# VectorE takes the weight sums of the first three feed-forward pairs, and the last row tile gets its residual from VectorE

## The chip, the cores and the metric

The kernel runs on one core of one Trainium2 chip. The metric is device time in microseconds (us). The kernel before took 1179.04 us as the median of three runs (1177.97 to 1402.14).

## The reference

The reference is one layer of a decoder trunk on 1024 positions of width 1024, all in float32. A first half computes latent attention, a short convolution and a state-space mixer from one normalised input and writes them through one output projection. What this document touches is the second half:

```
x = x + rms_norm(mixed, norm_mix_post)
h = rms_norm(x, norm_ffn_pre)
u = causal_dwconv(h @ ffn_w_up, ffn_conv_w) + ffn_conv_b      # 1024 -> 2 * 2816
gate, up = split(u)
x = x + rms_norm((silu(gate) * up) @ ffn_w_down, norm_ffn_post)
```

## The kernel before

Every float32 product is made of three TensorE products of rounded parts: a matrix is cast on ScalarE to a high part, the difference of matrix and high part is its low part, and high*high, high*low and low*high are summed in a PSUM bank. A low part is thus one elementwise subtraction per 128x1024 weight tile, after a cast.

**The up projection** works on pairs: pair j is gate tile j (`rg`) and up tile j (`ru`), each 128x1024 of weights. Instead of eight half products a pair takes seven, of sums and differences of weight halves (named 11, 12, S1, S2, S3, S4, 22) and of sums of activation halves (11, 21, T1, T2, T3, T4, 22), in the manner of Strassen and Winograd. So between load and product stand sums of weight halves (function `ew`, L1001), a cast on ScalarE, and the subtraction for the low part (L97 in `split_w`, L999 in `low`).

The first three pairs (j = 0, 1, 2; `NE` = 3) overlap the end of the first half, where rows 6 and 7 of the eight row tiles still pass through their norms (`norms`, L892). They go in steps over all three pairs: `pair_first` (L1040) makes the products 11 and 12 and gathers them in `ug`: ScalarE copies the first bank (L1045) and VectorE adds the second (L1048), which frees that bank. Then `sab_weights` (L1006) loads both tiles of the pair again, makes two sums of 128x512 in `ru`, and casts and lowers `ru`; S1 and S2 follow for all three pairs, first on one half of the columns, then on the other. Then `scd_weights` (L1013) loads the tiles a third time and makes the weights of S3, S4 and 22: four sums of 128x512 on VectorE, then casts and low parts, of which one is 128x512 (`hl_`) and one 128x1024 (`wlo`). In `sab_weights` the two sums and the low part of pairs 0 and 1 are on GpSimd (POOL) and those of pair 2 on VectorE; in `scd_weights` the two low parts of pairs 0 and 1 are on POOL and those of pair 2 on VectorE. The low parts of the first weights (`first_weights`, L972) are on POOL too.

The raw weight tiles rotate over three buffers (`raw` twice, `xraw` once), so the load of a tile waits on SyncE's queue until the low part or sum that last read its buffer is done.

The order of the instructions on each engine up to here is set by a planner that takes ready work by program order with costs of its own. From L1122 on TensorE, ScalarE, VectorE and SyncE follow the program's order (`by_hand`): pairs 3 to 21, then the down projection. POOL has nothing to do there but the last stores.

**The end.** The residual, x after the first half, was stored to the output rows by ScalarE's queue (`x2_st`, L925) long before. In the down projection row tile t is gathered in `acc[t]`. When a tile is complete, ScalarE squares its halves with a running sum (`squares`, L1357), VectorE and ScalarE make the reciprocal root (`scales`, L1361), VectorE multiplies by it and by the gain `gfin` (`finish`, L1369), and POOL issues a DMA (L1371) that adds the tile to the output rows in memory. Tiles 4 to 7 end one after the other at L1427 to L1433; for tile 7 the multiplication and the adding DMA go in two halves.

Of the kernel before, what the change touches and what calls it, by code (L numbers as in the profile page):

```python
# [8 lines left out]
F32 = mybir.dt.float32  # L9
# [4 lines left out]
ALU = mybir.AluOpType  # L14
# [3 lines left out]
D = 1024  # L18
# [26 lines left out]
def trunk(ctx: ExitStack, tc: tile.TileContext, x, xt, pos, cp, cst, amask, gains, wqkv, win, wqn, wqr, wkn,  # L45
          wv, wout, wup, wdn, out):
    nc = tc.nc
    pe, act, dve, pool, sp = nc.tensor, nc.scalar, nc.vector, nc.gpsimd, nc.sync

    def newpool(stack, name, bufs=1, **kw):  # L50
        if kw.get("space") is not DRAM:
            kw.setdefault("reuse_waits", "tile")
        return stack.enter_context(tc.tile_pool(name=name, bufs=bufs, **kw))
# [21 lines left out]
    def load_raw(src, w=1024):  # L75
        if more and more[2] % 3 == 2:
            raw = more[0].tile([128, 1024], F32, name="xraw")
        else:
            raw = wst.tile([128, 1024], F32, name="raw", bufs=2)
        if more:  # L80
            more[2] += 1
        sp.dma_start(out=raw[:, 0:w], in_=src)
        return raw
# [3 lines left out]
    def split_w(raw, w=1024, eng=None):  # L87
        if more and more[1] % 4 == 3:
            hi = more[0].tile([128, 1024], F32R, name="xhi")
            lo = more[0].tile([128, 1024], F32R, name="xlo")  # L90
        else:
            hi = wst.tile([128, 1024], F32R, name="whi", bufs=3)
            lo = wst.tile([128, 1024], F32R, name="wlo", bufs=3)
        if more:
            more[1] += 1
        act.copy(hi[:, 0:w], raw[:, 0:w])  # L96
        (eng or pool).tensor_tensor(out=lo[:, 0:w], in0=raw[:, 0:w], in1=hi[:, 0:w].bitcast(F32), op=ALU.subtract)  # L97
        return hi, lo
# [26 lines left out]
    def rsqrt_act(sp_, v, n, tag, bufs=2):  # L125

        y = sp_.tile([128, n], F32, name=tag + "_y", bufs=bufs)
        t = sp_.tile([128, n], F32, name=tag + "_t", bufs=bufs)
        act.activation(t, v, AF.Sqrt)
        dve.reciprocal(out=y, in_=t)  # L130
        dve.tensor_tensor(out=t, in0=y, in1=y, op=ALU.mult)
        dve.scalar_tensor_tensor(out=t, in0=t, scalar=-0.5, in1=v, op0=ALU.mult, op1=ALU.mult)
        dve.scalar_tensor_tensor(out=y, in0=t, scalar=1.5, in1=y, op0=ALU.add, op1=ALU.mult)
        return y
# [71 lines left out]
    with ExitStack() as g0:  # L206
# [8 lines left out]
        for k in range(KD):  # L215
# [12 lines left out]
            for c in parts:  # L228
                act.activation(hh[:, k, c], xr[:, c], AF.Copy, scale=g)
                dve.scalar_tensor_tensor(out=hl[:, k, c], in0=xr[:, c], scalar=g, in1=hh[:, k, c].bitcast(F32),  # L230
                                         op0=ALU.mult, op1=ALU.subtract)
# [37 lines left out]
    with ExitStack() as g2:  # L269
        st = newpool(g2, "st2")  # L270
        tb = st.tile([32, T], F32, name="tb")
# [16 lines left out]
        for i, n in enumerate((256, 128)):  # L288
            dve.scalar_tensor_tensor(out=v2[:, i, :], in0=cq_ss[:, i * NT:(i + 1) * NT], scalar=1.0 / n, in1=r2,
                                     op0=ALU.mult, op1=ALU.mult)  # L290
# [5 lines left out]
        for t in range(NT):  # L296
            dve.tensor_scalar(out=craw[:, t, 0:256], in0=craw[:, t, 0:256], scalar1=rc[:, t:t + 1], scalar2=None,
                              op0=ALU.mult)
            dve.tensor_scalar(out=craw[:, t, 256:384], in0=craw[:, t, 256:384], scalar1=rc[:, NT + t:NT + t + 1],
                              scalar2=None, op0=ALU.mult)  # L300
        for i in range(3):
            g = par("qn", i) if i < 2 else par("kvn")
            for hf in range(2):
                pt = bank()
                for q in range(4):
                    tr = pe.transpose(pt[:, q * 128:(q + 1) * 128], craw[:, hf * 4 + q, i * 128:(i + 1) * 128], ident)
                    if first_tr is None:
# [5 lines left out]
                                         op1=ALU.subtract)  # L313
# [66 lines left out]
    for d in (11, 9, 7, 5, 3, 1):  # L380
# [8 lines left out]
                             op0=ALU.mult, op1=ALU.mult)  # L389
# [13 lines left out]
    for i in range(6):  # L403
        u = in_tile(win[i], last_sq if i == 2 else None)
        if i == 1:
            tc.add_manual_dep(first_tr.ins, marks[2].ins.name,
                              mybir.DependencyInfo(mybir.DependencyClass.NoSync, mybir.DependencyReason.DATA),
                              reason="the norms of c_q and c_kv take that long")
        acc = ut.tile([128, T], F32, name="acc", bufs=1)
# [10 lines left out]
    with ExitStack() as g4:  # L420
        st = newpool(g4, "st4")
        tb = [st.tile([128, T], F32, name=f"tb{i}") for i in range(2)]
# [32 lines left out]
    for c in range(NT):  # L455
# [6 lines left out]
        for h in range(4):  # L462
            dve.scalar_tensor_tensor(out=dg[:, h, :], in0=aB[:, h, :], scalar=acs[:, c * 4 + h:c * 4 + h + 1],
                                     in1=maskT, op0=ALU.subtract, op1=ALU.add)
# [4 lines left out]
        for i in range(2):  # L469
# [3 lines left out]
                          in1=dtv[:, c, :].unsqueeze(2).broadcast_to([128, 4, 64]), op=ALU.mult)  # L473
# [6 lines left out]
        for g in range(2):  # L480
# [3 lines left out]
                          in0=psc[:, 0:256].rearrange("p (g l) -> p g l", g=2).unsqueeze(2).broadcast_to(  # L484
                              [128, 2, 2, 128]),
                          in1=dg.rearrange("p (g r) l -> p g r l", g=2), op=ALU.mult)
        if c > 0:
            Cd = sd.tile([128, 4, 128], F32, name="Cd")
            dve.tensor_tensor(out=Cd.rearrange("p (g r) l -> p g r l", g=2),
                              in0=Cm[:, :, cs].unsqueeze(2).broadcast_to([128, 2, 2, 128]),  # L490
                              in1=eB.rearrange("p (g r) l -> p g r l", g=2), op=ALU.mult)
# [19 lines left out]
        for i in range(2):  # L511
            dve.scalar_tensor_tensor(out=yz[:, i, cs], in0=xs[:, i, cs], scalar=par("dsk", i),
                                     in1=py[:, i * 128:(i + 1) * 128], op0=ALU.mult, op1=ALU.add)
# [3 lines left out]
        for i in range(2):  # L517
            pe.matmul(py[:, 256:258], sq[:, i, :], ones, start=i == 0, stop=i == 1)
        dve.tensor_scalar(out=vs[:, c:c + 1], in0=py[:, 256:257], scalar1=1.0 / 256, scalar2=EPS, op0=ALU.mult,
                          op1=ALU.add)  # L520
    rs = rsqrt(small, vs, NT, "rs")
    col_to_rows(rs, NT, small, rB2 := sd.tile([128, T], F32, name="rB2"), "r2")
    for i in range(2):
        dve.scalar_tensor_tensor(out=y[6 + i], in0=yz[:, i, :], scalar=par("sdn", i), in1=rB2, op0=ALU.mult,
                                 op1=ALU.mult)
# [3 lines left out]
    for i in range(2):  # L529
# [3 lines left out]
        acc = ut.tile([128, T], F32, name="acc", bufs=1)  # L533
# [266 lines left out]
    x2_st = {}  # L800
# [23 lines left out]
    H0, H1 = slice(0, 512), slice(512, 1024)  # L824
# [144 lines left out]
    def half(w, c):  # L969
        return [v_[:, c].rearrange("p (k c) -> p k c", k=4) for v_ in w]  # L970

    def first_weights(j, rg):  # L972
        ta = split_w(rg)
        return {"11": half(ta, H0), "12": half(ta, H1)}

    wts = [first_weights(j, load_raw(wup[j])) for j in range(NE)]
# [5 lines left out]
    def raws(j):  # L982
        ru = load_raw(wup[NJ + j])
        return load_raw(wup[j]), ru
# [10 lines left out]
    def half_split():  # L995
        return (ft.tile([128, 512], F32R, name="hh_", bufs=2), ft.tile([128, 512], F32R, name="hl_", bufs=2))

    def low(eng, lo, src, hi):
        eng.tensor_tensor(out=lo, in0=src, in1=hi.bitcast(F32), op=ALU.subtract)  # L999

    def ew(eng, dst, a_, b_, op):  # L1001
        eng.tensor_tensor(out=dst, in0=a_, in1=b_, op=op)  # L1002
# [3 lines left out]
    def sab_weights(w, rg, ru, eng):  # L1006

        ew(eng, ru[:, H0], ru[:, H0], ru[:, H1], ADD)
        ew(eng, ru[:, H1], ru[:, H0], rg[:, H0], SUB)
        tb = split_w(ru, eng=dve if w is wts[2] else pool)  # L1010
        w.update({"S1": half(tb, H0), "S2": half(tb, H1)})

    def scd_weights(w, rg, ru):  # L1013

        eng = dve if w is wts[2] else pool
        s1 = ft.tile([128, 512], F32, name="s1")
        ew(dve, s1, ru[:, H0], ru[:, H1], ADD)
        ew(dve, ru[:, H0], rg[:, H0], ru[:, H0], SUB)
        ew(dve, s1, s1, rg[:, H0], SUB)
        ew(dve, rg[:, H1], rg[:, H1], s1, SUB)  # L1020
        d_ = half_split()
        act.copy(d_[0], rg[:, H1])
        low(eng, d_[1], rg[:, H1], d_[0])
        c_ = split_w(ru, eng=eng)
        w.update({"S3": half(c_, H0), "22": half(c_, H1), "S4": half(d_, H0)})
# [51 lines left out]

    fst = [pair_first(j, wts[j]) for j in range(NE)]
    for j in range(NE):
        sab_weights(wts[j], *raws(j), pool if j < 2 else dve)  # L1080
    for nm in ("T1", "T2", "22", "T3", "T4"):
        if nm == "T4":
            put("T4", t4, 4)
# [42 lines left out]
    rg, ru = raws(NE)  # L1126
    for j in range(NE - 1, NJ):
# [38 lines left out]
        if more_:  # L1166
# [30 lines left out]
            if j < NJ - 2:  # L1197
                rg, ru = raws(j + 2)
# [21 lines left out]
    acc = [ab.tile([128, D], F32, name=f"acc{t}") for t in range(NT)]  # L1220
# [63 lines left out]
    def tok(ps, t, ol, or_, start, stop, more_):  # L1284
        ts = slice(t * 128, (t + 1) * 128)
        for i, (l_, r_) in enumerate(((ol[0], or_[0]), (ol[0], or_[1]), (ol[1], or_[0]))):
            pe.matmul(ps[t], l_[:, ts], r_[:, H1], start=start and i == 0, stop=stop and i == 2,  # L1287
                      skip_group_check=more_)
# [48 lines left out]
    fin = None  # L1337
# [10 lines left out]
    def gather(ps, t, row, c, copy):  # L1348
        dst = acc[row + t][:, c]
        if copy:  # L1350
            act.copy(dst, ps[t])
        else:
            ew(dve, dst, ps[t], dst, ADD)

    FULL = slice(0, 1024)
# [5 lines left out]
    def scales(t, n=1):  # L1361
        v = fin.tile([128, 4], F32, name="fv", bufs=2)[:, 0:n]
        ew(dve, v, ssd_[:, t:t + n, 0], ssd_[:, t:t + n, 1], ADD)
        dve.tensor_scalar(out=v, in0=v, scalar1=1.0 / D, scalar2=EPS, op0=ALU.mult, op1=ALU.add)
        return rsqrt_act(fin, v, n, f"fr{n}")

    def finish(t, r, *cs):
        for c in cs:
            dve.scalar_tensor_tensor(out=acc[t][:, c], in0=acc[t][:, c], scalar=r, in1=gfin[:, c], op0=ALU.mult,  # L1369
                                     op1=ALU.mult)  # L1370
            st_ = pool.dma_start(out=out[t * 128:(t + 1) * 128, c], in_=acc[t][:, c], accum_op=ALU.add)  # L1371
            tc.add_manual_dep(st_.ins, x2_st[t].ins.name,
                              mybir.DependencyInfo(mybir.DependencyClass.Sync, mybir.DependencyReason.DATA),
                              reason="the rows are added to what lies there")

    prepare_to(-2)
    act.copy(last[2][:, H0], b_last)
# [4 lines left out]
    for k, (bk_, q_, p_) in enumerate(steps):  # L1382
# [19 lines left out]
        if not ci and q_ == "P7" and p_ == ch[0]:  # L1402
# [3 lines left out]
            fin = newpool(ds_, "fin")  # L1406
            gfin = fin.tile([128, D], F32, name="gfin")
# [5 lines left out]
        if ci and q_ == "P7":  # L1413
# [4 lines left out]
            elif i == 2:  # L1418
                r = scales(0, 4)
# [2 lines left out]
                finish(i - 2, r[:, i - 2:i - 1], FULL)  # L1422

    ps = bank["b"]
    for t in range(4):
        squares(4 + t, H1)
    for t in range(4):  # L1427
        for p_ in ch:
            tok(ps, t, O[4, 0, p_], O[2, 1, p_], False, p_ == ch[-1], True)
        gather(ps, t, 4, H0, False)  # L1430
        squares(4 + t, H0)
        r = scales(4 + t)
        finish(4 + t, r, *((FULL,) if t < 3 else (H1, H0)))  # L1433
    by_hand.close()
    ds_.close()

# [81 lines left out]
```

## Time and profile before

| | |
|---|---|
| median of three runs | 1179.04 us |
| lowest run | 1177.97 us |
| profiled execution, own time | 1176.4 us |
| its span, first to last instruction | 1174.6 us |
| granted TensorE clock, mean | 0.988 |
| TensorE busy | 1126.3 us |
| VectorE busy | 887.6 us |
| ScalarE busy | 579.9 us |
| POOL busy | 167.7 us |

The profile is of one execution. Busy time is per engine; "idle before" is what an engine waited just ahead of an instruction, with what ended that wait. Times of the timeline count from the span's first instruction. A granted clock of 1.00 is 2.4 GHz, one of 0.50 is 1.2 GHz.

### The profile page before, as it was taken

What the parts mean: (1) busy time and instruction counts of PE and PEld (TensorE: products, weight loads), DVE (VectorE), ACT (ScalarE), POOL (GpSimd) and SP (SyncE); (2) the same over time, 40 slices, a digit from 0 to 9 for tenths busy, and PEclk for the clock granted to TensorE, in tenths of its full rate; (3) what the DMA queues carried; (4) which work ended last, traced back from release to release, by engine and by line L of the source; (5) the groups of instructions that cost most, each with busy time, mean ns of one, the idle gap of its engine ahead of it and who ended that gap; (6) DMA issues with size and microseconds to landing.
All of it is one profiled execution on the core that took longest, in us unless ns stands there. A gap on an engine that the chain in (4) does not pass through costs nothing.

```text
span 1174.6 us, 14711 instructions
## 1 busy us (share of the span) xinstructions
PE 1126.3 (96%) x5548; PEld 942.1 (80%) x5548; DVE 887.6 (76%) x1374; ACT 579.9 (49%) x931; POOL 167.7 (14%) x100
## 2 busy tenths in 40 slices
PE   9999999999999999979899999999999998999995
PEld 8778877788888877868688888888888887788884
DVE  4687378667889765876987777887878678779975
ACT  5743233157777744634544454444444444543542
POOL 2322211134424113341100000000000000000002
PEclk9999999999999999989999999999999999999998
DMA  8531151130111256551223132222222290560008
GB/s 270 190 91 45 36 167 41 48 96 10 37 28 28 72 207 198 188 175 40 90 90 108 55 107 74 88 90 73 90 72 90 70 360 26 190 232 1 1 4 140
DMA packets 42823, 118.01 MB, mean 100 GB/s; under 512 B 5392, under 2 KB 7040, under 8 KB 42400
## 3 DMA queue, kind: packets, MB, share of 16 engines
q1 hardware_dynamic: 37856, 104.36, 27.6%
q0 software_dynamic: 1296, 4.19, 2.2%
q10 hardware_dynamic: 3600, 8.52, 2.0%
q8 instruction: 43, 0.70, 0.3%
q14 instruction: 28, 0.23, 0.1%
HBM read 94.59 MB, written 22.47 MB: 100 GB/s over the span
## 4 chain that ended last, share of the span: by engine, by line
PE 63%; DVE 7%; issue 5%; DMA 4%; POOL 2%; ACT 2%; SPq 0%; POOLq 0%; ACTq 0%; DVEq 0%
PE cb L1032 26%; PE pb L1287 7%; PE pc L1287 5%; PE tp L1032 4%; PE S L104 2%; PE pt L705 2%; PE S L105 2%; PE S L106 2%; PE cb L105 2%; PE cb L104 2%; PE cb L106 2%; DMA raw<-in_wup 1%; PE po L721 1%; PE po L720 1%; DVE a L655 1%
## 5 line engine op out<-in xcount | busy, mean ns | idle before, releaser
L1032 PE MATMUL cb<-a,whi 128*128 128x512 f32 (+1 forms) x712 | 215.1, 384 | 5.2 <-DVE ug L1002 4.2
L1032 PEld LDWEIGHTS cb<-a,whi 128*128 128x128 f32 x712 | 133.3, 191 | 30.9 <-DVE ug L1002 4.6
L1032 PE MATMUL cb<-a,wlo 128*128 128x512 f32 (+1 forms) x356 | 136.7, 384 | 2.5 <-POOL wlo L97 2.5
L97 POOL TENSOR_TENSOR wlo<-raw,whi 128x1024 fp32r<-128x1024 f32 (+1 forms) x29 | 70.5, 2433 | 267.6 <-ACT whi L96 247.4
L1371 POOL DMA_DIRECT2D out<-acc x9 | 8.0, 907 | 596.7 <-DVE acc L1369 596.5
L106 PE MATMUL bk<-hh,wlo 128*128 128x512 f32 x224 | 89.3, 399 | 0.0
L104 PE MATMUL bk<-hh,whi 128*128 128x512 f32 x224 | 89.2, 398 | 0.0
L105 PE MATMUL bk<-hl,whi 128*128 128x512 f32 x224 | 89.0, 397 | 0.0
L1032 PEld LDWEIGHTS cb<-a,wlo 128*128 128x128 f32 x356 | 67.9, 191 | 15.9 <-POOL wlo L97 3.3
L363 DVE SCALAR_TENSOR_TENSOR cg<-ug,cpt,cg 128x1023 f32<-128x1023 f32 (+1 forms) x46 | 61.0, 1325 | 15.9 <-ACT cg L1114 12.9
L1032 PE MATMUL cb<-a,xhi 128*128 128x512 f32 (+1 forms) x248 | 72.7, 376 | 0.0
L96 ACT CAST whi<-raw 128x1024 fp32r<-128x1024 f32 (+1 forms) x33 | 33.8, 1025 | 65.5 <-PE bk L105 34.9
L363 DVE SCALAR_TENSOR_TENSOR cu<-uu,cpt,cu 128x1023 f32<-128x1023 f32 (+1 forms) x42 | 53.8, 1281 | 9.5 <-ACT cu L1114 8.8
L999 DVE TENSOR_TENSOR wlo<-raw,whi 128x1024 fp32r<-128x1024 f32 x35 | 42.7, 1222 | 13.3 <-ACT whi L1131 5.1
L1032 PEld LDWEIGHTS cb<-a,xhi 128*128 128x128 f32 x248 | 45.5, 188 | 8.4
L1114 ACT ACTIVATE cg<-ug,cpt 128x1024 f32<-128x1024 f32 x19 | 23.7, 1245 | 57.0 <-DVE ug L1002 54.8
L106 PEld LDWEIGHTS bk<-hh,wlo 128*128 128x128 f32 x224 | 42.2, 188 | 9.7 <-issue 0.4
L105 PEld LDWEIGHTS bk<-hl,whi 128*128 128x128 f32 x224 | 42.2, 188 | 9.4 <-issue 0.2
L104 PEld LDWEIGHTS bk<-hh,whi 128*128 128x128 f32 x224 | 42.2, 188 | 9.1
L1249 ACT CAST oh<-x 128x1024 fp32r<-128x1024 f32 x31 | 31.9, 1052 | 35.2 <-PE pb L1287 21.9
L1032 PE MATMUL cb<-a,xlo 128*128 128x512 f32 (+1 forms) x124 | 46.9, 378 | 1.4 <-DVE xlo L999 1.4
L999 DVE TENSOR_TENSOR ol<-x,oh 128x1024 fp32r<-128x1024 f32 x31 | 37.2, 1219 | 13.4 <-ACT oh L1249 13.3
(568 smaller groups left out, 3078.5 us busy)
## 6 DMA issues: line engine op xcount, KB each, us to landing
raw<-in_wup SPq DMA_DIRECT2D x35, 512.0 KB, 3.7
x<-g_d SPq DMA_DIRECT2D x44, 256.0 KB, 5.4
x<-in_wdn SPq DMA_DIRECT2D x44, 256.0 KB, 5.4
g_d<-uu SPq DMA_DIRECT2D x20, 512.0 KB, 2.9
xraw<-in_wup SPq DMA_DIRECT2D x18, 512.0 KB, 3.9
raw<-in_win SPq DMA_DIRECT2D x14, 512.0 KB, 3.5
raw<-in_wout SPq DMA_DIRECT2D x13, 512.0 KB, 4.2
xk<-in_x SPq DMA_DIRECT2D x8, 512.0 KB, 6.0
```

Of the source, the lines that this page charges most:

```text
L96: act.copy(hi[:, 0:w], raw[:, 0:w])
L97: (eng or pool).tensor_tensor(out=lo[:, 0:w], in0=raw[:, 0:w], in1=hi[:, 0:w].bitcast(F32), op=ALU.subtract)
L104: pe.matmul(ps, ah, bh, start=start, stop=False)
L105: pe.matmul(ps, ah, bl, start=False, stop=False)
L106: return pe.matmul(ps, al, bh, start=False, stop=stop)
L363: dve.scalar_tensor_tensor(out=dst[:, s:T], in0=u[:, 0:T - s], scalar=par(wname, i * width + width - 1 - s), in1=dst[:, s:T], op0=ALU.mult ...
L705: pe.transpose(pt[:, kz * 256 + jj * 128:kz * 256 + (jj + 1) * 128], P[jj][:, kb * 128:(kb + 1) * 128], ident)
L999: eng.tensor_tensor(out=lo, in0=src, in1=hi.bitcast(F32), op=ALU.subtract)
L1032: pe.matmul(ps[:, c], l_[:, k, :], r_[:, k, c], start=start and k == 0 and i == 0, stop=k == 3 and i == 2, skip_group_check=not start or c ...
L1114: act.activation(dst, u, AF.Identity, scale=par("fcw", i * 3 + 2), bias=par("fcb", i))
L1249: act.copy(o[0], src)
L1287: pe.matmul(ps[t], l_[:, ts], r_[:, H1], start=start and i == 0, stop=stop and i == 2, skip_group_check=more_)
```

## The change

In the up projection the sums and low parts of `sab_weights` for pairs 0 and 1, and the low parts of `scd_weights` for pairs 0 and 1, go from POOL to VectorE. At the end, the residual rows of tile 7 are loaded into a tile `x7` on SyncE's queue; VectorE multiplies the halves of `acc[7]` by the gain into a tile `g7` before the row's scale is known, then multiplies by the scale and adds `x7` in one instruction a half; the halves leave by ordinary stores on ScalarE's and SyncE's queues. Tiles 0 to 6 end as before.

```diff
     def sab_weights(w, rg, ru, eng):
         ew(eng, ru[:, H0], ru[:, H0], ru[:, H1], ADD)
         ew(eng, ru[:, H1], ru[:, H0], rg[:, H0], SUB)
-        tb = split_w(ru, eng=dve if w is wts[2] else pool)
+        tb = split_w(ru, eng=dve)
...
     def scd_weights(w, rg, ru):
-        eng = dve if w is wts[2] else pool
+        eng = dve
...
-        sab_weights(wts[j], *raws(j), pool if j < 2 else dve)
+        sab_weights(wts[j], *raws(j), dve)
...
+    def after_x2(t, d_):
+        tc.add_manual_dep(d_.ins, x2_st[t].ins.name, ..., reason="the residual's rows lie in the output")
...
     ps = bank["b"]
+    x7 = fin.tile([128, D], F32, name="x7")
+    after_x2(7, sp.dma_start(out=x7, in_=out[7 * 128:8 * 128, :]))
+    g7 = fin.tile([128, D], F32, name="g7")
     for t in range(4):
         squares(4 + t, H1)
     for t in range(4):
         for p_ in ch:
             tok(ps, t, O[4, 0, p_], O[2, 1, p_], False, p_ == ch[-1], True)
+        if t == 3:
+            ew(dve, g7[:, H1], acc[7][:, H1], gfin[:, H1], ALU.mult)
         gather(ps, t, 4, H0, False)
         squares(4 + t, H0)
-        r = scales(4 + t)
-        finish(4 + t, r, *((FULL,) if t < 3 else (H1, H0)))
+        if t < 3:
+            finish(4 + t, scales(4 + t), FULL)
+        else:
+            ew(dve, g7[:, H0], acc[7][:, H0], gfin[:, H0], ALU.mult)
+            r = scales(7)
+            for c, q_ in ((H1, act), (H0, sp)):
+                dve.scalar_tensor_tensor(out=g7[:, c], in0=g7[:, c], scalar=r, in1=x7[:, c], op0=ALU.mult, op1=ALU.add)
+                q_.dma_start(out=out[7 * 128:8 * 128, c], in_=g7[:, c])
```

## Rows read from the trace of the kernel before

**Rows 1.** Page, its head and part 1: busy us, share, instructions by engine.

```profile
span 1174.6 us, 14711 instructions
PE 1126.3 (96%) x5548; PEld 942.1 (80%) x5548; DVE 887.6 (76%) x1374; ACT 579.9 (49%) x931; POOL 167.7 (14%) x100
```

**Rows 2.** Waits of TensorE, 490 to 600 us: total, times, longest.

```profile
PE cb L1032 <- DVE ug L1002: 4.2, 1, 4.2
PE cb L1032 <- POOL wlo L97: 2.5, 2, 1.4
PE cb L1032 <- POOL hl__5468 L999: 1.5, 1, 1.5
PE cb L1032 <- DVE xlo L999: 1.4, 1, 1.4
...
PE cb L1032 <- ACT whi L96: 1.0, 1, 1.0
...
PE cb L1032 <- POOL hl__5425 L999: 0.7, 1, 0.7
```

**Rows 3.** Stretches: length, PE, PEld, DVE, ACT, POOL busy (count), granted clock, DMA.

```profile
519.00:523.10 4.10, 0.00 (x0) 0.00 (x0) 3.05 (x6) 3.22 (x10) 0.00 (x0) 0.78 0.90 342
523.10:528.20 5.10, 5.08 (x24) 5.08 (x25) 4.72 (x12) 1.92 (x4) 0.00 (x0) 0.51 0.57 175
528.20:531.80 3.60, 3.60 (x32) 3.60 (x32) 2.32 (x4) 0.37 (x1) 0.00 (x0) 1.00 0.17 68
549.00:556.00 7.00, 4.83 (x13) 3.35 (x14) 0.00 (x0) 0.14 (x1) 3.26 (x2) 0.76 0.44 150
...
566.00:587.00 21.00, 19.63 (x87) 15.78 (x86) 20.35 (x24) 14.53 (x16) 0.00 (x0) 1.00 0.28 94
```

**Rows 4.** Timeline of ScalarE: start, length, instruction, idle before.

```profile
514.01 1.05 ACT L96 CAST whi<-raw 128x1024 fp32r<-128x1024 f32 x1 [6.03 <-POOL raw L1002]
514.97 0.20 ACT L129 ACTIVATE rn_t<-v 128x2 f32<-128x2 f32 x1
...
523.97 1.05 ACT L96 CAST xhi<-xraw 128x1024 fp32r<-128x1024 f32 x1
```

**Rows 5.** Timeline of POOL, two low parts of pair 1.

```profile
515.14 2.39 POOL L97 TENSOR_TENSOR wlo<-raw,whi 128x1024 fp32r<-128x1024 f32 x1 [1.16 <-ACT whi L96]
...
561.72 2.25 POOL L999 TENSOR_TENSOR hl__5468<-raw,hh__5467 128x512 fp32r<-128x512 f32 x1
```

**Rows 6.** Timeline of VectorE, up projection.

```profile
515.40 2.16 DVE L131 TENSOR_TENSOR rn_t<-rn_y 128x2 f32<-128x2 f32 x1
...
520.63 0.69 DVE L1002 TENSOR_TENSOR xraw<-xraw,raw 128x512 f32<-128x512 f32 x1
...
525.05 1.22 DVE L97 TENSOR_TENSOR xlo<-xraw,xhi 128x1024 fp32r<-128x1024 f32 x1 [0.16 <-ACT xhi L96]
...
559.61 3.24 DVE L363 SCALAR_TENSOR_TENSOR cg<-ug,cpt,cg 128x1023 f32<-128x1023 f32 x1
```

**Rows 7.** Page, part 5: such a tap over the whole run, mean ns.

```profile
L363 DVE SCALAR_TENSOR_TENSOR cu<-uu,cpt,cu 128x1023 f32<-128x1023 f32 (+1 forms) x42 | 53.8, 1281 | 9.5 <-ACT cu L1114 8.8
```

**Rows 8.** Timeline of VectorE, the end (tile 7).

```profile
1162.86 0.68 DVE L1002 TENSOR_TENSOR acc<-pb,acc 128x512 f32<-128x512 f32 x1
1164.39 0.16 DVE L1002 TENSOR_TENSOR fv<-ssd 128x1 f32<-128x1 f32 x1 [0.85 <-ACT fjk L1359]
...
1165.79 1.41 DVE L1369 SCALAR_TENSOR_TENSOR acc<-acc,fr_y,gfin 128x512 f32<-128x512 f32 x2
```

**Rows 9.** Timeline of POOL, the last two adding DMAs.

```profile
1166.83 1.76 POOL L1371 DMA_DIRECT2D out<-acc  x2 [2.73 <-DVE acc L1369]
```

**Rows 10.** DMA issues: queue, count, KB each, median us from issue to landing.

```profile
g_d<-uu SPq DMA_DIRECT2D x20, 512.0 KB, 2.9
...
out<-acc POOLq DMA_DIRECT2D x2, 256.0 KB, 4.8
...
krope_d<-ks SPq DMA_DIRECT2D x1, 256.0 KB, 2.7
```

More of the change, by code (lines that the diff above doesn't have):

```diff
@@ L1365, in scales @@
         return rsqrt_act(fin, v, n, f"fr{n}")
+    def after_x2(t, d_):
+        tc.add_manual_dep(d_.ins, x2_st[t].ins.name,
+                          mybir.DependencyInfo(mybir.DependencyClass.Sync, mybir.DependencyReason.DATA),
+                          reason="the residual's rows lie in the output")
     def finish(t, r, *cs):
@@ L1370, in finish @@
                                      op1=ALU.mult)
[L1371 to L1374, printed above, removed]
+            after_x2(t, pool.dma_start(out=out[t * 128:(t + 1) * 128, c], in_=acc[t][:, c], accum_op=ALU.add))
     prepare_to(-2)
```

## The prediction

> **What bounds the kernel now.** First the page's head and busy times [rows 1]: TensorE is busy for 1126.3 of 1174.6 us. So time is to be had only where TensorE stands idle, runs at the low clock, or has ended. Both parts of the change lie at such places, and I read them one by one.
>
> TensorE's waits around the first three pairs [rows 2]: 4.2 us once for `ug` on VectorE, 2.5 us in two waits for POOL's `wlo`, 1.5 and 0.7 us for POOL's two `hl_`, 1.0 us for a cast, and 1.4 us for VectorE's `xlo`, the last just inside pair 3. Only the POOL waits name an engine that the change relieves; the largest names VectorE, which gets more work. So I followed it back. The stretches [rows 3] show it as 4.1 us without a matmul from 519.0, and behind it 24 products of half width in 5.08 us at a granted clock of 0.51, the 1.2 GHz level; the next 32 take 3.60 us at 1.00, that is 2.4 GHz. TensorE had been idle before the clock fell. ScalarE's timeline [rows 4] gives the cause: a cast of pair 1's weights held ScalarE for 6.03 us until POOL's sum was there at 514.01, and behind it in ScalarE's order stood the root `rn_t` of the last norm group (rows 6 and 7), at 514.97. The norm's VectorE chain, and the copies into `ug` that free a bank for TensorE, come after that root. One more delay is in the chain: a 128x2 multiplication on VectorE lasted 2.16 us, from 515.40 to 517.56 [rows 6], while its neighbours in the norm at 128x1 take 0.16 [rows 8]; POOL's low part ran from 515.14 to 517.53 [rows 5].
>
> The end [rows 8 to 10]: the last multiplications end at 1167.20, POOL issues the second adding DMA after the first, at 1166.83 + 0.88 = 1167.71, its kind lands 4.8 us after issue, at 1172.5, and 2.1 us more pass until the span ends at 1174.6.
>
> **The change part by part.** Both the engines and the queues are fixed by the edited lines, so that the change does not do what it says is ruled out. What is open is the order that the planner makes of the moved instructions.
>
> *Load on VectorE.* Moved are four sums and two low parts of 128x512 at 0.68 [rows 8] and four low parts of 128x1024 at 1.22 [rows 6]: 6 x 0.68 + 4 x 1.22 = 9.0 us. VectorE gets part back: the 128x2 step loses 2.0 us, and a tap of 3.24 us [rows 6] where such a tap takes 1.28 [rows 7] loses 2.0. So the net load is about 5.0 us, beside gaps: VectorE is wholly idle from 549 to 556 [rows 3].
>
> On this overlap the Trainium skill, SBUF — State Buffer, "Who interferes with whom", states that a VectorE instruction with two SBUF inputs and a GpSimd instruction reading SBUF share a port, and the second one waits out the first. The trace agrees, the short step ending 0.03 us after POOL's. By that rule both losses go; if they did not, the net load would be 9.0 us, and the forecast 2 us later by the norm's step alone.
>
> *Stretch 1, 509 to 531.* Without POOL's sum ahead of it the root can follow its own statistics, and the cast after it. I estimate both stalls gone: 4.2 us of waiting, and 5.08 − 24 x 3.60 / 32 = 2.4 us of low clock; 6.6 together. What is late next is pair 2's S1. TensorE reaches it at 519.0 + 24 x 0.11 = 521.7. Pair 2's second sum waits on a load that rotates through the same buffers; if it keeps its time, 520.63 + 0.69 = 521.3, the cast (now not queued until 523.97 behind the `ug` copies) ends at 522.4 and the low part at 523.6: 1.9 us of new waiting. I take 6.6 − 1.9 = **4.7 us**. Ends: 6.6 if the loads get earlier too, as each low part frees its buffer some 1.2 us sooner [rows 5, 6]; −7.2 by the rival below.
>
> *Stretch 2, 547 to 587.* Pair 0: 1.4 + 0.7 us of POOL waits go, since VectorE is idle there and its low parts are 2.39 − 1.22 = 1.2 and 2.25 − 0.68 = 1.6 us shorter [rows 5, 6, 8]; with them 4.83 x (1 − 0.76) = 1.2 us of low clock [rows 3]. Pair 1: 2.5 − 1.4 + 1.5 = 2.6 us of POOL waits; I leave 0.6 for a low part that stands behind half a tap [rows 7]: 2.0. The 1.0 us for the cast stays. That is 5.3. But from 566 to 587 VectorE is busy for 20.35 of 21.0 us [rows 3] and already makes TensorE wait 1.4 us for `xlo`. VectorE's own chain up to there gets only 0.1 us shorter (pair 1's low parts, 1.9 us, come in; 2.0 us of tap loss goes), TensorE's 2.0 us at pair 1; up to the difference of 1.9 comes back as a longer wait for `xlo`, and I take half, 0.9. I take 5.3 − 0.9 = **4.4 us**; ends 0 (all taken back there) and 6.5 (no waits left but the cast's 1.0).
>
> *The end.* VectorE has no idle time ahead of tile 7's gather at 1162.86, and `g7`'s first half is put in front of it: +0.68. The second half of `g7` fits into the 0.85 us in which VectorE waits for the squares [rows 8]: nothing; without that cover it costs 0.68. The last two VectorE steps keep their kind and length, so they end at 1167.88. Nothing is queued behind ScalarE's store, and behind SyncE's load of `x7` only the last store; that load has the whole second half of the down projection. A store of 256 KB lands 2.7 us after issue, one of 512 KB 2.9 [rows 10]: I take 2.7 for the same size, giving 1170.6 against 1172.5: **1.9 us**. Ends: a landing as slow as the adding DMA's 4.8 gives −0.2; one shorter by the same step as from 2.9 to 2.7 gives 2.1.
>
> The Trainium skill, DMA: Bandwidth & Descriptors, "Rules for kernel authors", advises against issuing a transfer as two halves, since both run on the same engines. By it one store of 512 KB after both steps would be as good: 1167.88 + 2.9 = 1170.8, 0.2 us behind the two. No run here shows that form.
>
> **Sum.** 4.7 + 4.4 + 1.9 = 11.0 us. The profiled execution's own time was 1176.4, 1.8 us over its span and 2.6 under the median; taken off 1176.4 it gives 1165.4, off the median of 1179.04, against which the change will be timed, **1168.0**.
>
> **Rivals.**
> *Only the end counts.* For it: VectorE is full from 566 to 587, and whatever the first stretches win can be waited away in front of `xlo`; TensorE's waits before that matter only as far as VectorE's own chain gets earlier. Against: VectorE's chain itself started late, behind products that waited for POOL, and it has 7 us of idle time at 549. Time: 1179.0 − 1.9 = 1177.1.
>
> *VectorE is blocked by loads.* The sums now sit on VectorE, whose order is fixed; if the planner puts pair 1's second sum and pair 2's ahead of the last group's norm steps, VectorE waits for loads that start only when pair 0's (then pair 1's) low part has freed a buffer, and that low part itself stands behind VectorE's work instead of running on POOL. For it: the same kind of wait held ScalarE for 6.03 us, and POOL's sum was what ended it. Against: work earlier in the program goes first among what is ready, and the norms come earlier. Price: two waits of about 3.6 us, which I estimate by the time from the low part's end at 517.53 to pair 2's sum at 520.63 plus its length (3.8) and round down, 7.2; stretch 2 gives nothing as the backlog goes on; 2.0 of the norm's step and 1.9 of the end come back: +3.3, **1182**. It decides against the change from 3.9 us of such waiting on.
>
> *Everything is won:* both stretches at their upper ends, 6.6 + 6.5 + 2.1 = 15.2: 1163.8.
>
> **How the numbers follow.** Forecast 0.55, only the end 0.20, blocked VectorE 0.15, everything 0.10. The range runs from 1161 (the best case, less the median's distance from quiet runs) to 1178 (past the end-only case); the blocked case is left out. Within 2% (1155.5 to 1202.6, about what a measurement of this kernel can tell from no change) lie all of them; I leave 0.02 on either side for an order of the planner's that I cannot see.
>
> **What would show it.** Right: no 4 us gap of TensorE near 519 and no stretch at 0.51 behind it; the root `rn_t` ahead of pair 1's cast; no 2 us step on VectorE in the norm; at most 2 us of waiting for pair 2's low part; TensorE's waits for low parts near 550 and 561 under 1 us together; the wait for `xlo` at pair 3 between 1 and 3 us; pair 4 starting some 9 us earlier; the last store issued some 0.7 us later after TensorE's last product than the last multiplication ended before, and landing in about 2.7. Wrong: VectorE idle ahead of a sum with a load as the cause; the same start of pair 4 as before; stores that take near 5 us; `x7` late.

## The result and the profile after

The kernel after takes 1166.10 us as the median of four runs (1164.91 to 1168.59), the kernel before 1178.68 us beside it; the ratio is 0.9898, with a 95% interval from 0.9875 to 0.9921. The execution of the kernel before that took 1402.14 us ran slow, and the ratio leaves it out. The forecast was 1168.0 us, so the time lies in the forecast's range, 1.9 us below its middle value. The profiled execution took 1166.94 us, at a mean granted clock of 0.99. Its page's head and part 1 answer to [rows 1]:

```profile
span 1165.2 us, 14701 instructions
PE 1125.9 (97%) x5548; PEld 942.4 (81%) x5548; DVE 889.1 (76%) x1386; ACT 580.1 (50%) x931; POOL 147.4 (13%) x88
```

TensorE's and VectorE's totals stay within 2 us of before, and POOL gives up 20. So the gain has to lie where TensorE stood still. To place it I cut the span at five starts in TensorE's timeline: the first product of the up projection (L1032), S4 of pair 0 (first product with `hh__5424`), pair 3's first product into `tp`, the last matmul, and the span's end. (`hh__5424` is the high part of pair 0's S4 weights; `tp` is a PSUM bank.) They stand at 497.04, 548.92, 586.08, 1162.27 and 1174.6 before, and at 497.09, 545.21, 579.56, 1155.82 and 1165.2 after. Below, the waits of a stretch are the sum of TensorE's listed waits in it, and "rest" is the stretch without them: work, and what the low clock adds to it.

| us | stretch 1 (S1, S2) | its waits, rest | stretch 2 (S3, S4, 22) | its waits, rest | pair 3 to last matmul | tail |
|---|---|---|---|---|---|---|
| before | 51.88 | 6.2, 45.7 | 37.16 | 7.0, 30.1 | 576.19 | 12.33 |
| after | 48.12 | 2.8, 45.3 | 34.35 | 3.8, 30.6 | 576.26 | 9.38 |
| difference | -3.76 | -3.4, -0.3 | -2.81 | -3.2, +0.4 | +0.07 | -2.95 |

They make 9.4 us. The medians differ by more, 12.6, since the profiled execution of before was 2.3 us under its median and that of after 0.8 over its own. Two versions below with the same up projection, e4 and e8, came out at ratios of 0.9912 and 0.9921, nearer to 9.4 us (0.992) than to 12.6. Nearly all of the gain in the two stretches is waiting; the rest hardly moved.

TensorE's waits from 490 to 600 us in the kernel after (engine, line, releaser: total, times, longest), against [rows 2]:

```profile
PE cb L1032 <- DVE xlo L999: 2.8, 1, 2.8
PE tp L834 <- DVE mxa L855: 1.9, 1, 1.9
PE cb L1032 <- DVE uu L1002: 1.0, 1, 1.0
PE tp L834 <- DVE a L838: 0.7, 2, 0.5
PE cb L1032 <- ACT hh__5424 L1022: 0.2, 1, 0.2
```

The wait of 4.2 us for `ug` is gone, and so is every wait for POOL. Others took their place: the wait for `xlo` has doubled, and those for `mxa` and for `uu` (VectorE's add that frees a bank of pair 0) are new. The stretches around the two longest show what they cost (length, PE, PEld, DVE, ACT, POOL busy, granted clock, DMA), against [rows 3]:

```profile
523.00:525.50 2.50, 0.65 (x6) 0.45 (x5) 2.50 (x5) 1.02 (x2) 0.00 (x0) 1.00 0.33 136
525.50:530.00 4.50, 4.48 (x25) 4.46 (x26) 4.50 (x7) 1.57 (x3) 0.00 (x0) 0.62 0.72 225
...
550.00:556.00 6.00, 5.00 (x23) 3.71 (x22) 6.00 (x9) 2.52 (x3) 0.00 (x0) 1.00 0.29 87
556.00:566.00 10.00, 10.00 (x45) 8.04 (x44) 9.71 (x12) 7.01 (x8) 0.00 (x0) 1.00 0.44 154
566.00:571.00 5.00, 2.77 (x13) 1.96 (x11) 5.00 (x7) 4.08 (x6) 0.00 (x0) 0.99 0.30 120
571.00:577.00 6.00, 5.44 (x13) 4.27 (x14) 6.00 (x7) 2.47 (x3) 0.00 (x0) 0.50 0.00 0
```

From 525.5 the clock is 0.62 on average, and from 571 it is 0.50, the 1.2 GHz level, for six microseconds; each time TensorE had just waited. In e8 below the same wait for `mxa` is followed by the full clock (again length, busy times, granted clock, DMA):

```profile
527.40:531.90 4.50, 4.42 (x36) 4.18 (x37) 4.50 (x7) 1.59 (x4) 0.00 (x0) 1.00 0.71 231
```

In the kernel after, VectorE has no gap at all in five of the six stretches.

Where the new wait for `mxa` comes from is in the timelines of the kernel after, first ScalarE's, against [rows 4], then VectorE's, against [rows 6] (start, length, instruction, idle before):

```profile
508.40 0.20 ACT L129 ACTIVATE rn_t<-v 128x2 f32<-128x2 f32 x1 [1.69 <-DVE v L900]
...
518.46 1.05 ACT L96 CAST whi<-raw 128x1024 fp32r<-128x1024 f32 x1 [2.39 <-issue]
519.41 0.20 ACT L129 ACTIVATE rn_t<-v 128x2 f32<-128x2 f32 x1
```

```profile
509.54 0.15 DVE L131 TENSOR_TENSOR rn_t<-rn_y 128x2 f32<-128x2 f32 x1
...
515.14 0.16 DVE L899 TENSOR_TENSOR v<-ss 128x2 f32<-128x2 f32 x1
517.69 0.69 DVE L1002 TENSOR_TENSOR raw<-raw 128x512 f32<-128x512 f32 x1 [2.39 <-DMA raw<-in_wup]
518.30 0.16 DVE L900 TENSOR_SCALAR v<-v 128x2 f32<-128x2 f32 x1
...
520.85 0.15 DVE L131 TENSOR_TENSOR rn_t<-rn_y 128x2 f32<-128x2 f32 x1
...
524.69 1.29 DVE L855 TENSOR_TENSOR mxa<-mxa,mxc 128x512 f32<-128x512 f32 x2
525.93 1.22 DVE L97 TENSOR_TENSOR xlo<-xraw,xhi 128x1024 fp32r<-128x1024 f32 x1
```

Rows 6 and 7 pass two norms here. The root of the first (508.40), which stood behind pair 1's cast before, now comes 10 us ahead of that cast (518.46), and its 128x2 step at L131 (509.54) lasts 0.15 us instead of 2.16. In the second norm it is otherwise: pair 1's first sum (517.69) waits 2.39 us for its load, and the norm's second step (518.30), ready since 515.30, stands behind it; its root (519.41) stands behind the cast. The sums of rows 6 and 7 for T1 (`mxa`, 524.69), for which TensorE waits, come at the end of that norm.

The end of the kernel after from its timeline, and behind it the last two stores from the DMA issues (KB each, median us to landing), against [rows 8 to 10]:

```profile
1156.41 0.69 DVE L1002 TENSOR_TENSOR g<-acc,gfin 128x512 f32<-128x512 f32 x1
...
1157.02 0.68 DVE L1002 TENSOR_TENSOR acc<-pb,acc 128x512 f32<-128x512 f32 x1
1157.73 0.69 DVE L1002 TENSOR_TENSOR g<-acc,gfin 128x512 f32<-128x512 f32 x1
...
1158.55 0.16 DVE L1002 TENSOR_TENSOR fv<-ssd 128x1 f32<-128x1 f32 x1
...
1159.94 1.42 DVE L1445 SCALAR_TENSOR_TENSOR g<-g,fr_y,x 128x512 f32<-128x512 f32 x2
1160.73 0.34 ACTq L1446 DMA_DIRECT2D out<-g  x1
1161.39 0.34 SPq L1446 DMA_DIRECT2D out<-g  x1
```

```profile
out<-g ACTq DMA_DIRECT2D x1, 256.0 KB, 2.1
out<-g SPq DMA_DIRECT2D x1, 256.0 KB, 2.2
```

The first `g` product stands ahead of the gather, the second lies in the wait for the squares, as costed. The last step ends 5.54 us after the last matmul's start, before it was 4.93. From there it is 3.84 us to the span's end: 2.2 for the landing, 1.6 behind it; before it was 7.4.

### The profile page after: what moved, and what is told of

Its sections match the earlier page's. It is cut to its first block, busy times and chain, and to the rows that moved or that the text cites. A ratio compares the mean times of both kernels' runs of the same rounds, so it can differ in the third digit from the quotient of the medians.

```text
span 1165.2 us, 14701 instructions
## 1 busy us (share of the span) xinstructions
PE 1125.9 (97%) x5548; PEld 942.4 (81%) x5548; DVE 889.1 (76%) x1386; ACT 580.1 (50%) x931; POOL 147.4 (13%) x88
## 4 chain that ended last, share of the span: by engine, by line
PE 66%; DVE 10%; DMA 4%; ACT 2%; issue 1%; SPq 0%; POOL 0%; DVEq 0%; ACTq 0%; POOLq 0%
PE cb L1032 29%; PE pb L1287 7%; PE pc L1287 5%; PE tp L1032 4%; PE pt L705 2%; PE S L104 2%; PE S L105 2%; PE S L106 2%; PE cb L105 2%; PE cb L106 2%; PE cb L104 2%; DMA x<-g_d 1%; PE po L721 1%; PE po L720 1%; DVE a L655 1%
## 5 line engine op out<-in xcount | busy, mean ns | idle before, releaser
L1032 PE MATMUL cb<-a,whi 128*128 128x512 f32 (+1 forms) x712 | 212.7, 381 | 1.1 <-DVE uu L1002 1.0
L1032 PEld LDWEIGHTS cb<-a,whi 128*128 128x128 f32 x712 | 131.4, 188 | 27.0 <-DVE uu L1002 1.4
L1032 PE MATMUL cb<-a,wlo 128*128 128x512 f32 (+1 forms) x356 | 135.2, 381 | 0.0
L97 POOL TENSOR_TENSOR wlo<-raw,whi 128x1024 fp32r<-128x1024 f32 (+1 forms) x25 | 60.4, 2418 | 227.1 <-ACT whi L96 227.0
L1032 PEld LDWEIGHTS cb<-a,wlo 128*128 128x128 f32 x356 | 66.8, 188 | 12.8 <-DVE wlo L97 0.3
L1032 PE MATMUL cb<-a,xhi 128*128 128x512 f32 (+1 forms) x248 | 76.1, 389 | 0.0
L1032 PEld LDWEIGHTS cb<-a,xhi 128*128 128x128 f32 x248 | 47.7, 197 | 8.7
L1032 PE MATMUL cb<-a,xlo 128*128 128x512 f32 (+1 forms) x124 | 48.1, 390 | 2.8 <-DVE xlo L999 2.8
```

Of the source, the lines that this page charges most:

```text
L1032: pe.matmul(ps[:, c], l_[:, k, :], r_[:, k, c], start=start and k == 0 and i == 0, stop=k == 3 and i == 2, skip_group_check=not start or c ...
```

## The experiments

Every ratio is to the kernel before on the same chip. The versions ran on different chips, so they are compared with each other by these ratios.

**One part alone.** Three kernels divide the change: e1 is before with the new end, e2 before with the edits for `sab_weights`, e3 before with that for `scd_weights`.

```diff
# e2, on before
-        tb = split_w(ru, eng=dve if w is wts[2] else pool)
+        tb = split_w(ru, eng=dve)
...
-        sab_weights(wts[j], *raws(j), pool if j < 2 else dve)
+        sab_weights(wts[j], *raws(j), dve)
# e3, on before (scd_weights)
-        eng = dve if w is wts[2] else pool
+        eng = dve
```

> The kernel before with the new end alone; the up projection is as before. If the end is worth what the two traces show from the last matmul to the span's end (11.9 us before, 9.0 after), this is 2.9 us faster than before and the whole change owes it a quarter. If the two parts depend on each other (the adding DMAs of tiles 4 to 6 end later than tile 7's stores when nothing else is earlier), it is under 1 us faster.

> The kernel before with the sums and low parts of S1 and S2 on VectorE alone; the low parts of S3, S4 and 22 of pairs 0 and 1 stay on POOL, the end as before. If each part has its own wait (my theory): TensorE reaches S4 of pair 0 some 3.7 us earlier, then waits for POOL's low parts as before: 3 to 4 us faster. Rival: VectorE's full stretch ahead of pair 3 takes back whatever arrives early: within 1 us of before, with the wait for xlo near 5 us.

> The kernel before with only the low parts of S3, S4 and 22 of pairs 0 and 1 moved to VectorE; sums and low parts of S1 and S2 stay on POOL, the end as before. My theory: TensorE's 4.2 us wait near 519 and the low clock behind it stay, POOL's waits of 4.7 us near 550 and 561 go, the wait for xlo grows from 1.4 to under 3: 2.5 to 4.5 us faster. Rival (the full stretch of VectorE takes all back): within 1 us of before.

| | ratio [95%] | stretch 1 | stretch 2 | tail |
|---|---|---|---|---|
| e1 | 0.9963 [0.9949, 0.9977] | 51.58 | 35.75 | 9.38 |
| e2 | 0.9958 [0.9942, 0.9974] | 48.15 | 35.55 | 11.77 |
| e3 | 0.9954 [0.9939, 0.9969] | 52.38 | 33.12 | 12.07 |

Each part gains by itself, in its own stretch: e1's tail is that of the kernel after, e2's stretch 1 too. *Only the end counts* falls: e2 and e3 keep the old end and are faster. The three gains of 0.37, 0.42 and 0.46% add to 1.25%, the upper end of the whole change's 0.79 to 1.25%. In time they are 4.4, 4.9 and 5.4 us, above the 2.9, the 3 to 4 and the middle of the 2.5 to 4.5 expected, but each interval reaches down to what was expected. That e1 and e2 show a shorter stretch 2 than the 37.16 us of before is no gain of theirs: their waits there are 7.0 and 6.8 us, and what differs is the low clock (last section).

e2 and e3 also hold the two overlaps with POOL apart. In e3 POOL still makes the S1/S2 low parts, and the norm's step is long; in e2 POOL makes the S3/S4 ones, and the tap is long, but not the norm's step. VectorE's timeline of e3, then of e2, each with the first norm's step and the tap:

```profile
514.27 2.16 DVE L131 TENSOR_TENSOR rn_t<-rn_y 128x2 f32<-128x2 f32 x1
...
556.72 1.28 DVE L363 SCALAR_TENSOR_TENSOR cg<-ug,cpt,cg 128x1023 f32<-128x1023 f32 x1
```

```profile
509.66 0.14 DVE L131 TENSOR_TENSOR rn_t<-rn_y 128x2 f32<-128x2 f32 x1
...
554.85 3.23 DVE L363 SCALAR_TENSOR_TENSOR cg<-ug,cpt,cg 128x1023 f32<-128x1023 f32 x1
```

So it is POOL's low part beside it that lengthens a VectorE instruction, each in its place. All four agree with the rule of the Trainium skill, SBUF — State Buffer, "Who interferes with whom". The kernel before has three more such instructions, two beside POOL's sums of pair 0 and one beside its `hl__5468`; instructions of their kind take 0.68 us elsewhere:

```profile
501.49 1.72 DVE L855 TENSOR_TENSOR mxb<-mxb 128x512 f32<-128x512 f32 x1
...
503.74 1.17 DVE L855 TENSOR_TENSOR mxb<-mxb 128x512 f32<-128x512 f32 x1
...
562.77 1.74 DVE L1002 TENSOR_TENSOR s<-xraw 128x512 f32<-128x512 f32 x1
```

The two at 501 and 503 cost TensorE waits of 0.8 and 0.7 us near 505, which stay in e3, where POOL keeps those sums, and are gone in e2 and in the kernel after.

**The queue or the adding DMA.** e4 sends the last two stores, plain, from POOL's queue; e8 makes one store of 512 KB of them.

```diff
# e4, on after
-            for c, q_ in ((H1, act), (H0, sp)):
+            for c, q_ in ((H1, pool), (H0, pool)):
# e8, on after
-            for c, q_ in ((H1, act), (H0, sp)):
+            for c in (H1, H0):
...
-                q_.dma_start(out=out[7 * 128:8 * 128, c], in_=g7[:, c])
+            sp.dma_start(out=out[7 * 128:8 * 128, :], in_=g7)
```

> The changed kernel with its two last stores issued on POOL's queue instead of ScalarE's and SyncE's; still ordinary stores. If the adding DMA was slow for its read of memory (4.8 us to land against 2.2 now), the stores land in 2 to 3 us here too and the loss is POOL's issue time: 0.9 to 1.8 us slower than the changed kernel. If POOL's queue itself lands late whatever it moves, 2.5 us or more slower, all of the end's gain gone.

> The changed kernel with one last store of 512 KB on SyncE's queue after both multiplications, instead of two halves on two queues. By the prediction's estimate 0.2 us later at the end; from the last matmul to the span's end 9.4 us in the changed kernel, so 9.4 to 9.7 here. If halves on two queues really overlap the first transfer with the second multiplication, up to 0.7 us later.

e4's ratio is 0.9912 [0.9893, 0.9932], its tail 9.49 us. Its stores in the DMA issues:

```profile
out<-g POOLq DMA_DIRECT2D x2, 256.0 KB, 2.4
```

From the same queue the adding ones took 4.8 [rows 10]. So POOL's queue costs 0.1 us of tail, less than the 0.9 to 1.8 expected; the addition was what took the time. e8's single store in the same view:

```profile
out<-g SPq DMA_DIRECT2D x1, 512.0 KB, 2.7
```

It lands 0.5 us slower than the halves, and e8's tail is 9.86 us, 0.5 more than with two stores. The ratio is 0.9921 [0.9901, 0.9942]; by time the two forms can't be told apart. The prediction had 0.2 us for it, by the rows. The rule of the Trainium skill that it cited (DMA: Bandwidth & Descriptors, "Rules for kernel authors") is about halves by partitions; here they are halves by columns, and the first leaves 0.66 us before the second is ready.

**The new waits.** e5 gives pair 3's `xlo` to POOL; e6 queues the sums of pairs 1 and 2 behind the last norm's root on VectorE, so that no load stands ahead of the norm; e7 does both.

```diff
# e5, on after
-            low(dve, ta[1], rg, ta[0])
+            low(pool if j == NE - 1 else dve, ta[1], rg, ta[0])
# e6, on after; last_root is the last norm's L133
-        sab_weights(wts[j], *raws(j), dve)
+        with tc.issue_after(last_root[0].ins) if j else ExitStack(): sab_weights(wts[j], *raws(j), dve)
```

> The changed kernel with one low part, xlo of pair 3, on POOL instead of VectorE. If TensorE's 2.8 us wait there, and the 0.50 clock behind it, come from VectorE's full stretch (my theory), POOL has the low part ready some 2.8 us after the cast's end near 566.6, so the wait falls to about 0.5 us and the clock stays at 1.00: 4 to 5 us faster than the changed kernel, a ratio to before near 0.986. Rival: POOL's instruction holds up VectorE's taps by as much as it relieves, and the wait only moves to the next low parts of pair 3: within 1.5 us of the changed kernel.

> The changed kernel with the sums and low parts of pairs 1 and 2 queued on VectorE behind the root of rows 6 and 7's second norm. My theory: VectorE's 2.4 us wait for a load stood in front of that norm and made TensorE wait 1.9 us for the sums of rows 6 and 7; with the norm first both go, and the low clock of 2.5 us behind them: 2 to 3 us faster than the changed kernel. Rival: the weights of pairs 1 and 2 come later by as much, and TensorE waits 2 us or more for a low part of S1 instead: no faster or slower.

> Both of the two edits before it. If each wait is its own, the gains add: 6 to 8 us faster than the changed kernel, a ratio to before near 0.984. If VectorE's chain to pair 3 is what counts alone, no faster than the version with xlo on POOL.

None of them gains, where 4 to 5, 2 to 3 and 6 to 8 us were expected; the rivals held: 0.9902 [0.9879, 0.9924], 0.9916 [0.9897, 0.9935] and 0.9922 [0.9904, 0.9939]. In e5 the wait for `xlo` falls to 0.3 us, but one of 3.1 us for the next low part takes its place. VectorE's timeline of e5, then POOL's, show why:

```profile
568.88 3.37 DVE L1002 TENSOR_TENSOR uu<-cg,cu 128x1024 f32<-128x1024 f32 x1
...
576.56 0.69 DVE L999 TENSOR_TENSOR hl__5603<-s,hh__5602 128x512 fp32r<-128x512 f32 x1
```

```profile
568.79 2.39 POOL L999 TENSOR_TENSOR xlo<-xraw,xhi 128x1024 fp32r<-128x1024 f32 x1 [68.28 <-ACT xhi L1131]
```

The multiplication took 1.22 us in the kernel after; beside POOL it takes 3.37. So VectorE saved 1.22 us for `xlo` and paid 2.15, ahead of `hl__5603`. In e6 the wait for `mxa` goes and one of 3.5 us for the cast of pair 1's weights comes, since its sum is now the late one: of the norm and the sum, whichever was second made TensorE wait. e7 has both new waits.

**VectorE's order.** What is left for `xlo` is that it need not be made beside or behind other work. e9 puts pair 1's taps and product, which nothing needs soon, behind pair 3's `xlo` and `hl` on VectorE; e10 behind all low parts of pair 3.

```diff
# e9, on after; late_gate issues only the two ScalarE starts of gate(1)
-        gate(j, ug, uu, ...)
+        (late_gate if j else gate)(j, ug, uu, ...)
...
             low(dve, s1w[1], s1, s1w[0])
+            if j < NE: taps(l1cg, l1[0], "fcw", 1, 3), taps(l1cu, l1[1], "fcw", NJ + 1, 3)
...
             act.copy(tc_[0], ru)
+            if j < NE: act.activation(l1cg, l1cg, AF.Silu), gated(1, *l1, l1cg, l1cu)
# e10: the same two lines, behind low(dve, td[1], rg, td[0]) and act.copy(n.uu[:, H1], n.c)
```

> The kernel after, but pair 1's taps (four of 1.28 us) and its product stand behind pair 3's low parts xlo and hl on VectorE instead of in front of them; nothing leaves VectorE and POOL gets nothing. Theory (VectorE's order decides how much of stretch 2 is won: with 2.5 us of taps less ahead of xlo its low part ends at about 569.1 instead of 571.5, and TensorE wants it at 568.8): the wait for xlo falls from 2.8 to under 0.8 us and the stretch at clock 0.50 behind it goes; since VectorE's total work up to pair 3's last low part stays (it ends near 582), up to 2 us come back there as a wait for wlo; from S4 of pair 0 to pair 3's first product into tp about 31 to 33 us against 34.4, ratio to the kernel before 0.987 to 0.990 (after: 0.9898). Rival (what is won at xlo is taken back whole at the next low part, as when xlo went to POOL): a wait of 2.5 us or more at hl or wlo, low clock behind it, ratio 0.990 to 0.992.

> As the run beside it, but pair 1's taps and product stand behind all low parts of pair 3 (6.4 us of VectorE's work are moved past the last one). Theory: the wait for xlo under 0.8 us, that for hl and wlo under 0.8 us as well, no stretch at clock 0.50 from 569 to 585, S4 of pair 0 to pair 3's first product into tp about 31 to 32.5 us, and nothing given back at pair 4: ratio 0.985 to 0.988, about 3 to 5 us less than the kernel after. Rival (VectorE's backlog only moves on: pair 4's low part or the bank behind ug comes late): a wait of 2 us or more for a low part or for ug between 580 and 600, ratio 0.989 to 0.992.

Both do at `xlo` what the theory said: a wait of 0.7 us, no stretch at the low clock behind it, stretch 2 in 29.41 and 29.43 us instead of 34.35. And both lose it again: 0.9916 [0.9897, 0.9935] and 0.9960 [0.9943, 0.9977], with 580.6 and 585.6 us from there to the last matmul instead of 576.3. Neither theory nor rival had the reason. e9's ratio is where its rival put it, but without the wait of 2.5 us for `hl` or `wlo` that the rival named; e10 shows a wait for `ug` as its rival said, at a higher price. TensorE's longest wait in e10 from 490 us on:

```profile
PE cb L1032 <- ACT ug L1146: 6.8, 1, 6.8
```

ScalarE's copy of `ug` stood behind the cast of pair 4, which waited 8.9 us for its load, and SyncE's queue shows why the load was late (both of e10):

```profile
589.69 1.05 ACT L1129 CAST whi<-raw 128x1024 fp32r<-128x1024 f32 x1 [8.94 <-DMA raw<-in_wup]
```

```profile
567.08 16.77 SPq L1071 DMA_DIRECT2D g_d<-uu  x2
583.91 1.26 SPq L82 DMA_DIRECT2D raw<-in_wup  x2
```

With the product its store had moved too, and pair 4's two loads stood behind it on the queue until VectorE had made pair 1's product. In e9 they left at 582.49 in the same way, and TensorE waited 1.6 us for the same copy, after 1.5 us for a cast and a low part of pair 3. I had counted the moved instructions on VectorE and not their DMA. e11 is e10 with that store behind the loads:

```diff
# e11, on e10
-                if j < NE: act.activation(l1cg, l1cg, AF.Silu), gated(1, *l1, l1cg, l1cu)
+                if j < NE: act.activation(l1cg, l1cg, AF.Silu), ew(dve, l1[1], l1cg, l1cu, ALU.mult)
...
                 rg, ru = raws(j + 2)
+            if j < NE: sp.dma_start(out=g_d[1], in_=l1[1])
```

> As the run before (pair 1's taps and product behind pair 3's last low part), but the store of pair 1's gated rows stands behind the loads of pair 4's weights on SyncE's queue instead of ahead of one of them. Theory (what undid that run is the queue alone: SyncE stood 16.8 us at the two stores, so both loads were issued only at 583.9 us, and the cast of pair 4 held ScalarE's copy of ug for which TensorE waited 6.8 us): both loads are issued by 578 us, the wait for ug of 6.8 us goes, no wait over 1 us between 572 and 620; the stretch up to pair 3's first product into tp stays at about 29.4 us and the rest goes back from 585.6 to about 576 to 577 us; ratio to the kernel before 0.984 to 0.988. Rival (VectorE's backlog is late by itself: pair 1's 6.4 us now stand ahead of pair 4's sums): a wait for ug or for pair 4's low part of 3 us or more remains, with the loads in time; ratio 0.990 to 0.995.

e11 takes 1162.87 us (1157.53 to 1165.02), ratio 0.9873 [0.9847, 0.9899]: the theory held, and this version beats both kernels in the median, though its interval overlaps that of the kernel after. The loads leave in time (SyncE's queue of e11), and the stretches behind `xlo` run at the full clock:

```profile
563.11 0.33 SPq L82 DMA_DIRECT2D raw<-in_wup  x1
566.88 0.33 SPq L1071 DMA_DIRECT2D g_d<-uu  x1
575.44 0.33 SPq L82 DMA_DIRECT2D raw<-in_wup  x1
583.35 0.33 SPq L1198 DMA_DIRECT2D g_d<-uu  x1
```

```profile
570.00:577.00 7.00, 7.00 (x31) 5.80 (x32) 6.64 (x8) 4.53 (x6) 0.00 (x0) 1.00 0.03 8
577.00:584.00 7.00, 7.00 (x32) 5.79 (x32) 6.82 (x7) 3.06 (x4) 0.00 (x0) 1.00 0.16 67
```

Stretch 2 is 29.38 us, of which 1.7 are waits and 27.7 the rest; from there to the last matmul it is 577.0, 0.8 more than after. VectorE does the same work as in the kernel after. Of 5.0 us won in the stretch, 2.1 are waits and 2.9 the low clock behind them; against e4 and e8, whose rest there is 29.1 us, the low clock's part is 1.4.

## Why the prediction was right

What the forecast said would go went in all three places, and e1 to e3 show that the parts gain where they were said to. What took its place in stretch 1 was not what it named, and the low clock was mis-sized. Step by step:

*POOL's sum holds the norm.* Shown for the sums and low parts together: without them on POOL the root comes ahead of pair 1's cast, the gap of 4.2 us at 519 is gone, in e2 and after, and it stays in e1 (4.1) and e3 (4.0).

*The two losses beside POOL.* Shown by e2 and e3, 2.0 us each as costed. But there were five and not two: the three lines shown with e2 and e3 cost VectorE 2.6 us more. So the net load on VectorE was too high in the forecast. By the page VectorE's busy time rose by 1.5 us, the two `g` products of the end included; the forecast's terms make 6.4.

*What is late next in stretch 1.* This step failed. I put pair 2's S1 there, with 1.9 us. It was the T1 sum of rows 6 and 7, by chance also with 1.9, behind a norm that stood 2.39 us behind pair 1's sum and its load. That is the blocked-VectorE rival's mechanism at one place and a third of its price, and one of the signs named for being wrong, VectorE idle ahead of a sum with a load as the cause, was there; e6 shows that undoing it only moves the wait.

*The low clock.* The failed size. In the sum of 11.0 us stood 2.4 and 1.2 of low clock that would end with its waits. The waits came out as forecast or better: 3.4 us in stretch 1 (2.3 forecast: 4.2 less 1.9; the two short ones near 505 went as well, unforeseen), 3.2 in stretch 2 (3.2 forecast: 4.4 less the 1.2). The second match is in part luck: all 4.7 us of POOL's waits went, not 4.1, and `xlo` took back 1.4, not 0.9; the cast's 1.0 went, and 1.0 for `uu` came. (For pair 0's `hl` I had read 2.25 us off pair 1's row; pair 0's took POOL 1.27, and its wait of 0.7 went all the same.) But the rest of the two stretches changed by -0.3 and +0.4, since a new wait of 1.9 and one of 2.8 us brought new low clock. I had priced what is late next by its wait alone. In stretch 2 e11 shows it: with that wait at 0.7 the rest falls from 30.6 to 27.7. I had also taken a low clock read off one execution for the fixed price of its wait. It is not: behind the same waits e1 lost 1.6 us where 2.4 were booked, and none where 1.2 were (last section). Over all versions, stretch 1's rest averages 45.7 us in the three with POOL's sums and 44.9 in the eight with them on VectorE in the planner's order; stretch 2's averages 29.2 in the three with POOL's low parts and 29.5 in the four with them on VectorE and the later order unchanged. So over both the rest fell by some 0.5 us, where 3.6 of low clock were booked.

*`xlo` gives back.* Right in place, short in size: from 1.4 to 2.8 us, where I had 2.3. e3 shows the same 2.8 with the S3/S4 edit alone, e2 keeps 1.4. Half of the possible give-back was too little. Pair 3's first product into `tp` came 6.5 us earlier, where the forecast had pair 4 start some 9 earlier.

*The end.* 2.95 us, where I had 1.9 and at most 2.1. The 0.68 ahead of the gather came as 0.61. The landing is 2.2 us and not 2.7, and the span ends 1.6 us behind it and not 2.1: I took the landing of an early store of another tile for this one, and carried over what followed the adding DMA. One store instead of two costs 0.5 us of tail (e8) and not 0.2.

The errors offset: too much low clock (3.7), too little waiting won in stretch 1 (1.1) and too little at the end (1.05). By profiles the sum is 9.4 and not 11.0. That the time still came out lower than forecast is the medians' distance from the two profiled executions, 2.3 and 0.8 us, and is luck, no gain of the change that a trace shows.

## What to carry to other kernels

A wait costs its length and often a low clock behind it; when the next late instruction is named, price that clock again for it before any is booked as won, and as a range from several executions. Before work is taken off a full engine, look whether its order can be changed: the work that nothing needs soon can go behind the part that TensorE waits for, as in e11, with no more work on any engine. And with an instruction that is moved goes its DMA: what stands behind that on the queue has to be looked up, for e10 and e11 differ in one store's place and by 9 us.

## What the runs showed of the hardware

The low clock behind the same wait is not the same in every execution. In stretch 1 the 4.5 us behind the wait of 1.9 us for `mxa` ran at 0.62 in the kernel after, e2 and e11, at 0.64 and 0.66 in e5 and e4, and at 1.00 in e8, e9 and e10; the 5.1 us behind the wait of 4.0 to 4.2 us for `ug` ran at 0.51 before, 0.50 in e3 and 0.69 in e1. Before and e1 have the same instructions and the same six waits in stretch 2 (7.0 us), yet the stretch took 37.16 and 35.75 us, and the 7 us around pair 0's two waits ran at 0.76 and 1.00; behind the wait for `xlo` of 2.8 us the clock from 575 to 580 was 0.73 in the kernel after and 0.99 and 1.00 in e8 and e4, whose order there is the same. What decides between these is open. So 1.4 us of such a stretch is not the change's, and one profile of each kernel does not settle a difference of that size. Where the clock is 1.00 over all of stretch 2, its rest is 28.7 us with six waits (e1, e2) and 27.7 with two (e9 to e11): I estimate from this that a wait costs TensorE some 0.25 us beyond its listed length. The adding DMA of 256 KB takes twice a plain one's time from the same queue, 4.8 against 2.4 us.
